# Announcing carry copies by the Exp that follows them, in a running log-sum-exp kernel

**Chip, cores, metric.** One core of a Trainium2 chip. The metric is the device time of one execution in microseconds; medians of several runs are quoted, and the profile is of one execution, whose span is some 1.7 us shorter than the device time. A run counts as slow when it is over 1.5% above the fastest run of the same kernel.

## The reference

A running log-sum-exp along the sequence, for 8 x 4096 x 2048 float32:

```python
out[:, 0, :] = x[:, 0, :]
for t in range(1, S):
    mx = np.maximum(out[:, t - 1, :], x[:, t, :])
    out[:, t, :] = mx + np.log(np.exp(out[:, t - 1, :] - mx) + np.exp(x[:, t, :] - mx))
```

It is the logarithm of a prefix sum of exp(x), and the kernel computes it so.

## The kernel before

The work is 64 tiles of 512 sequence rows (128 partitions, 4 rows each, 2048 columns, 4.19 MB). Six buffers `ti` hold tiles, each worked on in place: load, Exp, prefix sum, Ln, store. Everything is done in two column halves, h = 0 and 1. The last row of a tile is carried into the next through the tile `rs`: ACT copies partitions 96 to 127 into `rs`, then VectorE overwrites all but partition 127 with the new tile's sums of rows, and a matmul with a triangle turns `rs` into the offsets that VectorE adds ("join"). So VectorE's write of `rs` must come after ACT's copy; this order is what the change re-announces.

```python
# SyncE: loads
take(sp, stored[n], 16)                 # wait for the buffer's store, subtract
load(x_v[...], n)                       # ... loaded[n] += 16

# ACT
def exp(n, h, rows=slice(0, R)):
    t = ti[n % NI]
    if h == 0:
        take(act, loaded[n % NI], 16)   # an event instruction: wait and subtract
    act.activation(t[:, rows, half(h)], t[:, rows, half(h)], ACT.Exp).then_inc(exps[h], 1)

def copy(n, h, turn):
    act.activation(
        rs[P - 32:, half(h)], ti[n % NI][P - 32:, R - 1, half(h)], ACT.Copy
    )._wait_ge(joined[h], turn + 1).then_inc(moved, 1)
    event(act, [(moved, 2 * turn + h + 1)], [(copied[h], "sem-add-imm", 1)])

def step(n, turn, early=False):
    copy(n - 1, 0, turn)
    if early:                           # only for the last tile
        ln(n - 1, 0)
    exp(n, 0)
    exp(n, 1)
    copy(n - 1, 1, turn)
    if not early:
        ln(n - 1, 0)
    ln(n - 1, 1)                        # then the store of tile n - 1

# VectorE
def local(n, h):                        # sums of rows, three adds
    dve.tensor_add(...)._wait_ge(exps[h], n + 1).then_inc(chain[h], 1)
    dve.tensor_add(...)._wait_ge(chain[h], 3 * n + 1).then_inc(chain[h], 1)
    dve.wait_ge(copied[h], n + 1)
    dve.tensor_add(rs[:P - 1, cols], ...)._wait_ge(chain[h], 3 * n + 2).then_inc(sums[h], 1)

def join(n, h):                         # add the offsets from PSUM, two adds
    dve.tensor_add(...)._wait_ge(ahead[h], n + 1).then_inc(chain[h], 1)
    dve.tensor_add(...)._wait_ge(chain[h], 3 * n + 3).then_inc(joined[h], 1)
# per tile: local(n, 0), local(n, 1), join(n, 0), join(n, 1)
# ... (matmuls, loops over tiles, semaphore clean-up, launch)
```

The softmax here doesn't subtract the row's maximum and nothing guards it: scores larger than these inputs give would overflow.

## Time and profile before

| | before |
|---|---|
| median of the first three runs | 1250.54 us (1250.41 to 1250.74) |
| VectorE, ACT busy | 84%, 84% |
| two DMA queues, share of 16 engines | 49.9% + 49.8% |
| bytes moved, mean rate | 536.96 MB, 430 GB/s |
| store to store on ACT, first 290 us / later | 17.26 us / 19.4 us |

A line of a timeline is: start in us, duration, engine, source line, operation, output<-input, count (neighbours are merged, so "x2" with 7.12 us are two Exp halves of 3.6 us), and in brackets the idle time before it with its releaser. "ACTq" is ACT's sequencer, here issuing a store or taking a semaphore. The prediction below shows the lines.

### The profile page before, as it was taken

How to read it: one execution, taken by the hardware profiler on the slowest of the kernel's cores; microseconds unless marked ns; L12 is line 12 of the kernel's file. 1: busy time of each engine (PE TensorE's matmuls, PEld its weight loads, DVE VectorE, ACT ScalarE, POOL GpSimd, SP SyncE). 2: the span in 40 equal slices, each digit the busy share in tenths (PEclk: the TensorE clock that was granted, in tenths of full speed). 3: DMA queues.
4: the chain of work that ended last, by engine and by line, in shares of the span. 5: the costliest groups of instructions: out<-in, count | busy, mean ns of one | idle time of the engine just before them, and what ended most of it. 6: DMA issues, size and time to landing. Idle time of an engine off the chain costs nothing. (4 is left out here: it accounts for less than half of the span.)

```text
span 1249.0 us, 3085 instructions
## 1 busy us (share of the span) xinstructions
PE 385.3 (31%) x512; PEld 131.3 (11%) x512; DVE 1044.3 (84%) x640; ACT 1046.2 (84%) x385; POOL 1.0 (0%) x7
## 2 busy tenths in 40 slices
PE   1332333323323323233232331423323234142230
PEld 0110111101101101011010010101101101010010
DVE  4999999998888888888888888888888888888881
ACT  3999999998888888888888888888888888888892
POOL 0000000000000000000000000000000000000000
PEclk9666666666667576666665756666667565666665
DMA  9999999999999999999999999999999999999998
GB/s 403 420 437 434 425 434 435 434 434 428 432 436 437 433 428 432 435 436 433 429 432 434 437 433 428 432 436 436 433 430 431 436 436 433 430 430 437 436 432 348
DMA packets 18726, 536.96 MB, mean 430 GB/s; under 512 B 2080, under 2 KB 2080, under 8 KB 2080
## 3 DMA queue, kind: packets, MB, share of 16 engines
q1 hardware_dynamic: 9360, 268.44, 49.9%
q10 hardware_dynamic: 9360, 268.44, 49.8%
q8 instruction: 4, 0.07, 0.0%
q14 instruction: 2, 0.02, 0.0%
HBM read 268.44 MB, written 268.44 MB: 430 GB/s over the span
## 5 line engine op out<-in xcount | busy, mean ns | idle before, releaser
L215 PE MATMUL ps<-rs,before 128*128 128x512 f32 (+1 forms) x512 | 385.3, 905 | 831.7 <-DVE rs L240 831.0
L142 ACT ACTIVATE ti<-ti 128x4096 f32<-128x4096 f32 (+1 forms) x128 | 452.5, 3582 | 109.2 <-ACTq L63 109.2
L155 ACT ACTIVATE ti<-ti 128x4096 f32<-128x4096 f32 x129 | 456.3, 3583 | 12.9 <-DVE ti L250 4.6
L246 DVE TENSOR_TENSOR ti<-ti,ps 128x3072 f32<-128x3072 f32 x128 | 428.8, 3350 | 10.6 <-PE ps L215 10.3
L233 DVE TENSOR_TENSOR ti<-ti 128x1024 f32<-128x1024 f32 x128 | 156.4, 1222 | 155.9 <-ACT ti L142 155.9
L215 PEld LDWEIGHTS ps<-rs,before 128*128 128x128 f32 (+1 forms) x512 | 131.3, 285 | 1084.8 <-DVE rs L240 975.1
L148 ACT ACTIVATE rs<-ti 32x1024 f32<-32x1024 f32 x126 | 132.6, 1052 | 52.9 <-DVE ti L250 39.1
L240 DVE TENSOR_TENSOR rs<-ti 127x1024 f32<-127x1024 f32 x128 | 156.8, 1225 | 4.4
L250 DVE TENSOR_TENSOR ti<-ti 128x1024 f32<-128x1024 f32 x128 | 156.8, 1225 | 4.4
L236 DVE TENSOR_TENSOR ti<-ti 128x1024 f32<-128x1024 f32 x128 | 156.8, 1225 | 4.4
L184 ACT ACTIVATE ti<-ti 128x4096 f32<-128x4096 f32 x1 | 3.6, 3616 | 6.3 <-ACTq L63 6.3
L35 ACT ACT_TABLE_LOAD x1 | 1.3, 1283 | 0.8 <-PEq L283 0.8
L107 POOL TENSOR_SCALAR_AFFINE_SELECT before<-before 128x128 f32<-128x128 f32 x1 | 0.3, 294 | 0.1
L101 POOL TENSOR_SCALAR_AFFINE_SELECT before<-before 128x128 f32<-128x128 f32 x1 | 0.3, 294 | 0.1
L98 POOL MEMSET before<- 128x128 f32 x1 | 0.2, 205 | 0.5 <-SPq L81 0.5
L283 POOL MEMSET const-bfloat16-1.0<- 128x1 bf16 x1 | 0.1, 102 | 0.0
L283 POOL MEMSET const-uint8-127<- 128x1 uint8 x1 | 0.1, 102 | 0.0
L283 POOL MEMSET const-float32-0.0<- 128x1 f32 x1 | 0.1, 99 | 0.3 <-issue 0.3
L283 POOL MEMSET const-float32-1.0<- 128x1 f32 x1 | 0.1, 99 | 0.0
## 6 DMA issues: line engine op xcount, KB each, us to landing
ti<-in_x_dram SPq DMA_DIRECT2D x63, 4096.0 KB, 26.5
out_dram<-ti ACTq DMA_DIRECT2D x63, 4096.0 KB, 54.6
ti<-in_x_dram SPq DMA_DIRECT2D x2, 2048.0 KB, 9.5
out_dram<-ti ACTq DMA_DIRECT2D x2, 2048.0 KB, 18.1
```

Of the source, the lines that this page charges most:

```text
L35: nc.scalar.preload_act_table_set("natural_log_exp_and_others")
L142: act.activation(t[:, rows, half(h)], t[:, rows, half(h)], ACT.Exp).then_inc(exps[h], 1)
L148: act.activation(rs[P - 32:, half(h)], ti[n % NI][P - 32:, R - 1, half(h)], ACT.Copy)._wait_ge(joined[h], turn + 1).then_inc(moved, 1)
L155: act.activation(t[:, rows, half(h)], t[:, rows, half(h)], ACT.Ln).then_inc(logs, 1)
L184: act.activation(ti[0][:, 0:2, :], ti[0][:, 0:2, :], ACT.Exp)
L215: m = pe.matmul(ps[n % 2][:, sl], before[:k, :], rs[:k, sl], start=True, stop=True,)
L233: dve.tensor_add(t[:, 1, cols], t[:, 0, cols], t[:, 1, cols])._wait_ge(exps[h], n + 1).then_inc(chain[h], 1)
L236: dve.tensor_add(t[:, 2, cols], t[:, 1, cols], t[:, 2, cols])._wait_ge(chain[h], 3 * n + 1).then_inc(chain[h], 1)
L240: dve.tensor_add(rs[:P - 1, cols], t[:P - 1, 2, cols], t[:P - 1, 3, cols])._wait_ge(chain[h], 3 * n + 2).then_inc(sums[h], 1)
L246: dve.tensor_add(t[:, 0:3, cols], t[:, 0:3, cols], ps[n % 2][:, cols].unsqueeze(1).to_broadcast([P, 3, HALF]),)._wait_ge(ahead[h], n + 1). ...
L250: dve.tensor_add(t[:, 3, cols], t[:, 2, cols], t[:, 3, cols])._wait_ge(chain[h], 3 * n + 3).then_inc(joined[h], 1)
L283: nc = _bacc.Bacc("TRN2", target_bir_lowering=False, num_devices=1)
```

## The change

The intent is to have fewer instructions for synchronization. Where the Exp half comes behind the copy of the same half on ACT, the Exp's own semaphore already tells VectorE that the copy is done. So the second copy is moved in front of the second Exp, and the event instruction, the semaphore `copied` and VectorE's wait for it go. The Ln halves, which overwrite what the copies read, now wait for the copies' own semaphore `moved`.

```diff
-        exps, chain, sums, ahead, joined, copied = (
+        exps, chain, sums, ahead, joined = (
 ...
                     )._wait_ge(joined[h], turn + 1).then_inc(moved, 1)
-                    event(act, [(moved, 2 * turn + h + 1)], [(copied[h], "sem-add-imm", 1)])
 ...
-                def ln(n, h, rows=slice(0, R)):
+                def ln(n, h, ready, turn, rows=slice(0, R)):
                     ...
-                    ).then_inc(logs, 1)
+                    )._wait_ge(ready, turn).then_inc(logs, 1)
 ...
                     if early:
-                        ln(n - 1, 0)
+                        ln(n - 1, 0, moved, 2 * turn + 1)
                     exp(n, 0)
+                    copy(n - 1, 1, turn)
                     exp(n, 1)
-                    copy(n - 1, 1, turn)
                     if not early:
-                        ln(n - 1, 0)
-                    ln(n - 1, 1)
+                        ln(n - 1, 0, moved, 2 * turn + 1)
+                    ln(n - 1, 1, moved, 2 * turn + 2)
 ...
-                    dve.wait_ge(copied[h], n + 1)
 ...
-                        take(dve, copied[h], tiles)
```

(Cut: GpSimd's first increments of `copied`, and the two waits for `joined` at the end, which move into the Ln calls.)

More of the change, by code (lines that the diff above doesn't have):

```diff
@@ L89 @@
         loaded, stored = sems("loaded", NI), sems("stored", NI)
-        exps, chain, sums, ahead, joined, copied = (
-            sems(s, 2) for s in ("exps", "chain", "sums", "ahead", "joined", "copied")
+        exps, chain, sums, ahead, joined = (
+            sems(s, 2) for s in ("exps", "chain", "sums", "ahead", "joined")
         )
@@ L110, in _ @@
                 ).then_inc(shaped, 1)
-                for h in range(2):
-                    g.sem_inc(copied[h], 1)
             @block.sync
@@ L198, in _ @@
                 turn = NT - 1 - first
-                act.wait_ge(joined[0], turn + 1)
-                ln(NT - 1, 0)
-                act.wait_ge(joined[1], turn + 1)
+                ln(NT - 1, 0, joined[0], turn + 1)
                 done = 2 * turn + 1
                 for rows in LAST:
-                    ln(NT - 1, 1, rows)
+                    ln(NT - 1, 1, joined[1], turn + 1, rows)
                     done += 1
```

## The prediction

> **What bounds the kernel now.** I read the page first, then the list of waits, then the ACT timeline of one tile in the middle, then stretches of time at the end. The work is 64 tiles of 4.19 MB, each loaded, worked on in place in one of six buffers, and stored.
>
> ```profile
> span 1249.0 us, 3085 instructions
> ...
> PE 385.3 (31%) x512; PEld 131.3 (11%) x512; DVE 1044.3 (84%) x640; ACT 1046.2 (84%) x385; POOL 1.0 (0%) x7
> ...
> DMA  9999999999999999999999999999999999999998
> ...
> q1 hardware_dynamic: 9360, 268.44, 49.9%
> q10 hardware_dynamic: 9360, 268.44, 49.8%
> ```
>
> The reader is to see that no engine is above 84%, while the DMA row is full in 39 of 40 slices and the two queues (loads, stores) together took 49.9 + 49.8 = 99.7% of the time of the 16 DMA engines. 536.96 MB in 1249.0 us is 430 GB/s. The DMA is the bound.
>
> ```profile
> DVE ti L233 <- ACT ti L142: 155.9, 64, 15.2
> ...
> ACT ti L142 <- ACTq L63: 109.2, 63, 2.4
> ```
>
> The columns are us in total, times, longest. Line 63 is the helper that takes a semaphore; in front of an Exp that semaphore is the one of the load. So ACT waits 109 us for loads, and VectorE in turn 156 us for the Exp: slack of both engines.
>
> ```profile
> 305.76 0.34 ACTq L173 DMA_DIRECT2D out_dram<-ti  x1
> 306.15 1.05 ACT L148 ACTIVATE rs<-ti 32x1024 f32<-32x1024 f32 x1 [0.55 <-DVE ti L250]
> 309.51 7.12 ACT L142 ACTIVATE ti<-ti 128x4096 f32<-128x4096 f32 x2 [2.31 <-ACTq L63]
> 316.66 1.05 ACT L148 ACTIVATE rs<-ti 32x1024 f32<-32x1024 f32 x1
> 317.83 7.12 ACT L155 ACTIVATE ti<-ti 128x4096 f32<-128x4096 f32 x2
> 325.12 0.34 ACTq L173 DMA_DIRECT2D out_dram<-ti  x1
> ```
>
> One tile on ACT, mid-kernel: first carry copy, 2.31 us for the load, both Exp halves, second copy, both Ln halves, store. From store to store it is 325.12 - 305.76 = 19.36 us. The DMA needs 2 x 4.194 MB / 433 GB/s (the rate in the stretch from 290 to 1200 us) = 19.4 us for a tile. They agree: the transfers set the pace. Until about 290 us it is otherwise: the six loads given at the start are ahead, ACT runs from store to store in 17.26 us (61.70 to 78.96) with only 0.2 us of load wait, and the DMA share is 1.00 all the same (433 GB/s from 60 to 290 us), because stores pile up behind it.
>
> ```profile
> ti<-in_x_dram SPq DMA_DIRECT2D x63, 4096.0 KB, 26.5
> out_dram<-ti ACTq DMA_DIRECT2D x63, 4096.0 KB, 54.6
> ```
>
> The last column is the median from issue to landing: 26.5 + 54.6 = 81.1 us, or 81.1 / 19.4 = 4.2 tiles in transfer at any time. Six buffers make 116 us a round, so 35 us are left for the arithmetic of a tile. The store queue is some 2.8 tiles deep: a store given a microsecond later waits a microsecond less.
>
> **What the Trainium skill says.** "Perfetto Trace Analysis", section "Identifying the Most-Contended Engine": for DMA one should judge by the bandwidth used, as occupancy of 16 engines misleads. Here both say the same, 430 GB/s and 99.7%. "DMA: Bandwidth & Descriptors", section "Where 436 GB/s comes from", gives 435.2 GB/s as the ceiling of the ports, and says that between HBM and SBUF about 358 GB/s of HBM bind before it. The trace agrees with the first (430 mean, slices up to 437) and contradicts the second. The same page, section "Issuing engines are not separate DMA queues", says transfers issued by several engines share the 16 DMA engines; the shares of the two queues above, adding to 99.7%, agree. "VectorE: DVE Perf Modes", section "The DRAIN you can't avoid", measured that a semaphore after each operation costs nothing extra there. The trace agrees for VectorE: the adds of lines 233, 236 and 240 start at 313.16, 314.42 and 315.68, so the gap in front of line 240, where the wait to be removed stands, is the same 0.03 us as in front of line 236, where none stands.
>
> **The change part by part.**
> (a) VectorE loses 128 waits for the copies. By the row just read each costs 0.00 us. It also loses some subtractions at the end of each round of six tiles. Gain on VectorE: about nothing.
> (b) ACT loses 126 event instructions behind the copies. Copy to Ln: 316.66 + 1.05 = 317.71 to 317.83, a gap of 0.12 us where back-to-back ACT work has 0.02 to 0.03. So about 0.1 us each, two a tile, 63 tiles: 126 x 0.1 = 12.6 us of ACT idle. The one before the first Exp lies inside the load wait (or merges with it: 0.21 us where no load is awaited). None of it is on the path: ACT then waits longer for the load.
> (c) The second copy moves from behind the second Exp half to in front of it. Its total work on ACT is the same (1.05 us). The first Exp ends when it did, the second ends 1.05 + 0.03 = about 1.1 us later, the Ln halves start where they did, less the 0.1 of (b). So the stores of a tile in the steady part are issued at the same time or 0.1 us sooner.
> (d) VectorE feels the later second Exp. Its three adds of half 0 start when the first Exp ends and take about 3.7 us; the next half was ready at once (3.56 us after), and will be ready 1.08 us later, so VectorE idles about 0.9 to 1.0 us there. The joins move 1 us later. Is it paid for? In VectorE's timeline of the same tile the join of half 0 ends at 304.80 + 1.22 = 306.02 against a load at 309.4: 3.4 us, less the copy's 1.05, are room. And the join of half 1 ends at 309.33 + 1.23 = 310.56; with 1.0 us it is 311.6, before the first Exp's end at 313.1, where the moved copy needs it. So nothing slips further: VectorE waits 1.0 us less before half 0 and 1.0 us more before half 1.
> (e) In the first part, where the engines set their own pace, a new loop closes: second Exp, adds of half 1 (3.75), join of half 0 (4.6), copy (1.05 and 0.1 to 0.2 of hand-over), first Exp (3.6), copy (1.08), second Exp (3.6) = 17.8 to 17.9 us against 17.26 now. That is still below the DMA's 19.4. The read-ahead is used up more slowly: it was 230 us / 17.26 = 13 tiles at 2.1 us gained each; at 1.5 to 1.6 us gained, about 18 tiles, to some 380 us. The DMA stays full, so 0 us.
> (f) The end. The last tile's second Exp, the joins and the two last stores come about 1.0 us later.
>
> ```profile
> 1225.95 0.34 ACTq L173 DMA_DIRECT2D out_dram<-ti  x1
> ...
> 1228.27 0.34 ACTq L173 DMA_DIRECT2D out_dram<-ti  x1
> ```
> ```profile
> 1200.00:1228.00 28.00, 5.48 (x8) 1.85 (x8) 19.69 (x12) 22.72 (x9) 0.00 (x0) 0.63 1.00 432
> 1228.00:1249.00 21.00, 0.00 (x0) 0.00 (x0) 0.00 (x0) 0.24 (x1) 0.00 (x0) 0.50 0.72 311
> ```
>
> The last two numbers of a stretch are DMA share and GB/s. After 1228 us, 21 x 311 = 6.5 MB still move, and from 1225.95 to 1228 some 2 x 0.43 = 0.9 MB; the two last stores are 4.2 MB together. So when the first of them was issued, 6.5 + 0.9 - 4.2 = 3.2 MB stood before it, 7.5 us of transfer. A delay of 1.0 us uses part of this and leaves no hole.
> Sum: (a) 0, (b) 0, (c) 0, (d) 0, (e) 0, (f) 0. The time stays at 1250.5 us.
>
> **Rivals.**
> First, ACT as the bound, as its 84% and the short chain at the end (ACT and DVE work back to 1183 us) might suggest: then 12.6 us of removed gaps would show, 1250.5 - 12.6 = 1238 us, 1% less. Against it: the 109 us that ACT waits for loads, and the full DMA row.
> Second, the moved copy as a new serial wait: if joins of half 1 came after the first Exp, ACT would stand and both engines would fall into one chain. At my 17.9 us a tile there are 1.5 us of room; had I missed over 1.5 us a tile the kernel would be slower by 64 us for each further one: at 20.5 us a tile it would be about 1250 + 64 x 1.1 = 1320 us. For it speaks only that the new loop alternates between the engines; its terms are all measured, and an error of 1.5 us in six is unlikely.
> Third, the end: if the last stores were not backed by a queue, the 1.0 us of (f) would be added whole: 1251.5 us.
> Fourth, another mix of loads and stores changes the DMA rate. The slices vary from 425 to 437 GB/s; a shift of 0.2% of the mean would be 2.5 us either way. I can't derive a direction.
>
> **Range and chances.** I take 1250.5 us. The runs of before spread by 0.3 us; the third and fourth rival give 1 to 2.5 us. Range 1248.5 to 1253.0. Faster by over 2% would need under 1225.5, a mean of 438 GB/s even without any start and end, above every slice of the row: 0.005. Slower by over 2% means the second rival: 0.015. Within 2%: 0.98.
>
> **What would show it.** The DMA row stays full with 430 GB/s over the span. VectorE's waits for the Exp (line 233) rise from 64 to about 127 times with a sum still near 156 us, the new ones of about 1 us. The copy-to-Ln gap of 0.12 us is gone. ACT's wait for loads in mid-kernel stays at 2.3 us; the first part runs at 17.8 to 17.9 us a tile and lasts till about 380 us. The last store is issued about 1 us later with the span the same. Wrong would be: holes in the DMA row, a load wait near zero in mid-kernel, or waits of the second copy for the join of half 1.

## The result

The changed kernel is correct. It took 1250.34 us (median of four runs: 1250.27, 1250.32, 1250.35, and one slow, 1269.64); the kernel before, on the same chip, 1250.47 us. The ratio of the fast runs is 0.9999, with a 95% interval of 0.9979 to 1.0019. A ratio here is the mean time of one kernel's fast runs over that of the other's in the same rounds, so not quite the ratio of the medians.

The page of the changed kernel, its span, DMA row and DMA total:

```profile
span 1248.6 us, 2807 instructions
...
DMA  9999999999999999999999999999999999999998
...
DMA packets 18726, 536.96 MB, mean 430 GB/s; under 512 B 2080, under 2 KB 2080, under 8 KB 2080
```

There are 278 instructions less than the 3085 of before, and the DMA row is as full. Its waits (us in total, times, longest):

```profile
DVE ti L229 <- ACT ti L138: 168.3, 127, 15.4
...
ACT rs L147 <- DVE ti L245: 92.1, 63, 10.2
ACT ti L138 <- ACTq L63: 75.6, 45, 1.7
```

The kernel before had, for the wait of the first copy:

```profile
ACT rs L148 <- DVE ti L250: 39.1, 53, 10.5
```

VectorE waits for an Exp 127 times instead of 64. ACT's first copy waits for the join 92.1 us instead of 39.1, and its Exp for loads 75.6 instead of 109.2: part of the slack has moved from the load wait to the join wait. The ACT timeline of one tile in mid-kernel:

```profile
714.07 0.34 ACTq L171 DMA_DIRECT2D out_dram<-ti  x1
715.23 1.05 ACT L147 ACTIVATE rs<-ti 32x1024 f32<-32x1024 f32 x1 [1.32 <-DVE ti L245]
717.99 3.62 ACT L138 ACTIVATE ti<-ti 128x4096 f32<-128x4096 f32 x1 [1.71 <-ACTq L63]
721.63 1.05 ACT L147 ACTIVATE rs<-ti 32x1024 f32<-32x1024 f32 x1
722.71 3.62 ACT L138 ACTIVATE ti<-ti 128x4096 f32<-128x4096 f32 x1
726.23 7.11 ACT L153 ACTIVATE ti<-ti 128x4096 f32<-128x4096 f32 x2
733.50 0.34 ACTq L171 DMA_DIRECT2D out_dram<-ti  x1
```

Store to store is 733.50 - 714.07 = 19.43 us, the same as before within the scatter of single tiles. The load comes 717.99 - 714.07 = 3.92 us after the store's issue (in the kernel before, from the lines in the prediction: 309.51 - 305.76 = 3.75), and from there to the next store it takes 15.51 us (before: 15.61). Only what lies inside is arranged differently. In the first part the stores come at 61.73, 79.47, 97.22 and so on, 17.74 us apart, up to about 345 us.

The stretches at the end of the changed kernel (last two numbers: DMA share and GB/s), and its last two stores:

```profile
1200.00:1228.00 28.00, 5.83 (x9) 1.85 (x8) 21.62 (x13) 21.35 (x8) 0.00 (x0) 0.68 1.00 431
1228.00:1249.00 21.00, 0.00 (x0) 0.00 (x0) 0.00 (x0) 2.43 (x2) 0.00 (x0) 0.50 0.73 315
```
```profile
1228.55 0.34 ACTq L171 DMA_DIRECT2D out_dram<-ti  x1
...
1230.88 0.34 ACTq L171 DMA_DIRECT2D out_dram<-ti  x1
```

The last stores are issued 2.6 us later than before, and the span still ends 0.4 us earlier.

### The profile page after: what moved, and what is told of

It is laid out like the page before. It is cut to its first block, busy times and chain, and to the rows that moved or that the text cites. A ratio compares the mean times of both kernels' runs of the same rounds, so it can differ in the third digit from the quotient of the medians.

```text
span 1248.6 us, 2807 instructions
## 1 busy us (share of the span) xinstructions
PE 418.3 (33%) x512; PEld 133.3 (11%) x512; DVE 1045.1 (84%) x640; ACT 1046.2 (84%) x385; POOL 1.0 (0%) x7
## 5 line engine op out<-in xcount | busy, mean ns | idle before, releaser
L211 PE MATMUL ps<-rs,before 128*128 128x512 f32 (+1 forms) x512 | 418.3, 964 | 801.3 <-DVE rs L235 801.2
L138 ACT ACTIVATE ti<-ti 128x4096 f32<-128x4096 f32 (+1 forms) x128 | 459.4, 3590 | 77.6 <-ACTq L63 75.6
L147 ACT ACTIVATE rs<-ti 32x1024 f32<-32x1024 f32 x126 | 132.6, 1052 | 93.6 <-DVE ti L245 92.1
```

The costliest lines, as they stand in the source:

```text
L147: act.activation(rs[P - 32:, half(h)], ti[n % NI][P - 32:, R - 1, half(h)], ACT.Copy)._wait_ge(joined[h], turn + 1).then_inc(moved, 1)
L211: m = pe.matmul(ps[n % 2][:, sl], before[:k, :], rs[:k, sl], start=True, stop=True,)
```

## The experiments

The theory under test: the transfers pace the kernel, the change makes the loop of the engines longer (17.26 to 17.74 us a tile), and the transfers hide that. The main rivals: the two parts cancel (moving costs what dropping events gains); the engines' loop already paces, or never matters; the end is a chain of engines.

| run | us, median | runs | ratio to before (95%) |
|---|---|---|---|
| move alone | 1251.38 | 5 | 1.0006 (0.9993 to 1.0019) |
| events of half 0 alone | 1250.83 | 6 | 1.0010 (0.9998 to 1.0021) |
| changed, one extra copy a tile | 1250.69 | 4 | 1.0000 (0.9986 to 1.0015) |
| changed, two extra copies a tile | 1306.38 | 4 | 1.0445 (1.0430 to 1.0460) |
| stores cut: before | 1146.12 | 4 | 0.9163 |
| stores cut: changed | 1169.82 | 4 | 0.9353 |
| stores cut: move alone | 1187.86 | 4 | 0.9496 |
| stores cut: events of half 0 alone | 1135.01 | 4 | 0.9074 |
| changed, end later by 2 dummies | 1251.42 | 4 | 1.0015 (0.9998 to 1.0032) |
| changed, end later by 5 dummies | 1252.27 | 7 | 1.0011 (0.9997 to 1.0025) |
| changed, end later by 8 dummies | 1258.12 | 4 | 1.0059 (1.0042 to 1.0075) |
| transfers alone | 1247.71 | 4 | 0.9976 (0.9959 to 0.9992) |

### Each part alone

The move without dropping anything:

```diff
                     exp(n, 0)
-                    exp(n, 1)
                     copy(n - 1, 1, turn)
+                    exp(n, 1)
```

> The kernel before with the second carry copy moved in front of the second Exp half; the event instructions and VectorE waits stay. Theory (transfers bind, both parts of the change are off the path): 1250.4 us within 0.1%, the DMA row full, and up to some 350 us a pace of about 18.0 us a tile (the 17.74 us of the changed kernel plus some 0.2 to 0.3 us of event gaps that now lie in the loop). Rival (two parts that cancel: the move costs and the dropped events pay for it): slower than before by about 126 x 0.1 = 12 us, near 1262 us.

And the dropping where no move is needed, for half 0:

```diff
-                    event(act, [(moved, 2 * turn + h + 1)], [(copied[h], "sem-add-imm", 1)])
+                    if h == 1:
+                        event(act, [(moved, 2 * turn + 2)], [(copied[1], "sem-add-imm", 1)])
...
-                    dve.wait_ge(copied[h], n + 1)
+                    if h == 1:
+                        dve.wait_ge(copied[1], n + 1)
```

(Cut: the first increment and the subtractions of `copied` for half 0, and a wait for `moved` in front of the early Ln of the last step.)

> The kernel before with event and wait dropped for half 0 alone, where the Exp half already stands behind the copy; the order of instructions is untouched. Theory (transfers bind): 1250.4 us within 0.1%; in the first part about 17.1 us a tile instead of 17.26. Rival (cancelling parts): the dropped events gain 63 x 0.1 to 0.2 us, so 1238 to 1244 us.

Both take the time of the kernel before. The stores of the first part came 18.02 us apart with the move alone and 17.08 us with the events of half 0 gone, as expected, and neither shows in the end. So the two parts don't cancel; each is hidden by itself, as the runs with stores cut, below, show with the price of each. The second kernel had two longer runs, 1252.16 and 1255.5 us, beside four between 1250.38 and 1251.14 (see the end of the section on the end).

### How much room the loop has

One or two needless copies of the carry's size behind the moved copy, into a spare tile:

```diff
+                    for j in range(EXTRA if h == 1 else 0):
+                        act.activation(
+                            spare[P - 32:, :], ti[n % NI][P - 32:, R - 1, half(1)], ACT.Copy
+                        )._wait_ge(moved, PER * turn + 2 + j).then_inc(moved, 1)
```

(Cut: the spare tile, and `PER`, the number of copies a tile, in the other waits for `moved`.)

> The changed kernel with one needless carry-sized copy (1.05 us) a tile behind the moved copy, so the loop of the engines grows from 17.74 to about 18.9 us a tile, still under the 19.43 us of the transfers. Theory: 1250 to 1252 us. Rival (the loop ACT - VectorE - ACT is already what paces the steady part): slower by 63 x 1.1 = 69 us, near 1320 us.

> The same with two needless copies a tile: loop about 20.0 us, now over the 19.43 us of the transfers. Theory: the bound changes over, stores at 20.0 us a tile from the first at 44 us: 44 + 62 x 20.0 + some 25 for the end = about 1309 us (1300 to 1320), and the DMA row no longer full. Rival (engines never on the path, whatever they cost): 1250 us. Rival (loop paces already): 1250 + 63 x 2.2 = 1389 us.

The first run paid 1.09 us a tile (18.83 us from store to store for the first 53 steps, then 19.4 us for the eight that follow) and lost nothing. The second ran at 19.91 us a tile and lost 4.45%. The DMA totals of the page tell which side each is on, first one extra copy, then two:

```profile
DMA packets 18726, 536.96 MB, mean 430 GB/s; under 512 B 2080, under 2 KB 2080, under 8 KB 2080
...
ACT ti L141 <- ACTq L66: 6.1, 9, 1.3
```
```profile
DMA packets 18726, 536.96 MB, mean 412 GB/s; under 512 B 2080, under 2 KB 2080, under 8 KB 2080
...
ACT ti L141 <- ACTq L66: 1.2, 1, 1.2
```

With two copies a load is awaited once in the whole kernel, and the rate falls to 412 GB/s. That wait is at the start. With one copy, eight of the nine waits come after the 53 steps at 18.83 us: through these the engines spaced the stores, with no wait for a load, and the total still did not grow. So a load wait near zero is no sign of a loss by itself; the transfers that were queued ahead have to be used up first. The two runs bracket the turning point between 18.83 and 19.91 us. It is not the 19.43 us of the transfers: the second run lost 1306.38 - 1250.69 = 55.7 us over 62 steps, 0.90 us a step, so an estimate from it is 19.91 - 0.90 = 19.0 us. (The kernels without a loss take 18.9 us a step in the mean of these 62, as their first steps are quicker.) This refutes both rivals about the loop: that it paced already, and that it never matters.

### The change where the transfers don't pace

The stores of all but the last tile carry only half of the rows; the results are wrong (rows of the output stay unwritten). All else is as in the four kernels named.

```diff
-                def store(n, dst, done, rows=slice(0, R)):
+                def store(n, dst, done, rows=slice(0, 2)):
```

> The kernel before, storing only half of the rows of all tiles but the last (a wrong result on purpose), so that a tile needs about 14.6 us of transfers and the engines set the pace throughout. Theory: the pace of the first part of the trace, 17.26 us a tile plus 0.74 us every six tiles, holds to the end: 44.4 + 62 x 17.38 + 12.7 + 10 = about 1145 us (1138 to 1152).

> The changed kernel with the same cut of the stores. Theory (the change lengthens the loop of the engines and the transfers hid it): 17.74 us a tile: 44.4 + 62 x 17.74 + 13.9 + 10 = about 1168 us (1160 to 1176), 2% slower than the kernel before with the same cut. Rival (the change is neutral on the engines too): the same as the kernel before with the cut, 1145 us. Rival (it makes the engines faster, by the 12.6 us of dropped gaps): 1133 us.

> Only the moved copy, events and waits kept, stores cut. Theory: all of the loss is from the move, and the dropped events win a part back: loop about 18.0 us a tile, about 1185 us (1178 to 1192), slower than the changed kernel with the cut. Rival (the loss in the first part comes from dropping the events): about 1145 us.

> Only the half-0 events and waits dropped, no move, stores cut. Theory: the gap between first copy and first Exp falls from 0.21 to about 0.03 us, ACT paces at 17.08 us a tile plus 0.74 every six: about 1134 us (1128 to 1142), the fastest of the four. Rival (an event costs nothing, as waits on VectorE do): 1145 us.

All four hit their ranges. Without the cover of the transfers the change costs 1169.82 - 1146.12 = 23.7 us (2.1%). Most of it is 0.36 us a step and not 17.74 - 17.26 = 0.48: in the kernel before every sixth step takes some 17.95 us, so its mean over 62 steps is 17.38 us, while in the changed kernel nearly all take 17.74 us. The move alone costs 41.7 us; dropping the events in the moved order wins 18.0 us of that back. Dropping the half-0 events without the move wins 11.1 us and is the fastest of the four. The gap on ACT between the first copy and the Exp shows where it is won; first the kernel before, then the half-0 one, both with stores cut:

```profile
705.98 1.05 ACT L148 ACTIVATE rs<-ti 32x1024 f32<-32x1024 f32 x1 [0.55 <-DVE ti L250]
707.24 7.12 ACT L142 ACTIVATE ti<-ti 128x4096 f32<-128x4096 f32 x2 [0.21 <-ACTq L63]
```
```profile
715.87 1.05 ACT L147 ACTIVATE rs<-ti 32x1024 f32<-32x1024 f32 x1 [0.55 <-DVE ti L251]
716.95 3.62 ACT L141 ACTIVATE ti<-ti 128x4096 f32<-128x4096 f32 x1
```

705.98 + 1.05 = 707.03, so the Exp stood 0.21 us behind the copy; without the event it is 0.03 us. 62 tiles x 0.18 us = 11.2 us, the whole gain. The taking of the load semaphore, which stands in both, then shows no cost beyond this 0.03 us.

### The end

Needless copies of 2048 elements into a free PSUM tile in front of the last Ln pieces of the changed kernel delay its last two stores. The edit, for two, five or eight of them (k):

```diff
+                for j in range(k):
+                    act.activation(
+                        ps[0][:].rearrange("p (a b) -> p a b", a=2),
+                        ti[(NT - 1) % NI][:, 0:2, half(1)], ACT.Copy
+                    )._wait_ge(*((joined[1], turn + 1) if j == 0 else (pad, j))).then_inc(pad, 1)
                 for rows in LAST:
```

> The changed kernel with two needless copies of 2048 elements into PSUM on ACT in front of the last Ln quarter tiles, some 4 us, so that the two last stores are issued some 4 us later. Theory (transfers queued at the end cover a delay of about 4.9 us, worked out for the changed kernel as 6.3 MB still to move at 1228.55 us less the 4.2 MB of the two last stores): 1250 to 1251 us. Rival (the end is a chain of engines and the last stores count at once): 1254.4 us.

> The same with eight needless copies, some 15.5 us. Theory: 4.9 us of it are covered, the rest counts: about 1261 us (1258 to 1264). Rival (end chain counts at once): 1266 us. Rival (the end is covered far more): 1250 us.

With two, the first of the last stores was issued 3.7 us later (1232.24), and the profiled run took 1250.34 us with the span of the changed kernel, 1248.6 us. The other three runs took 1251.19, 1251.65 and 1255.16 us, so the median of 1251.42 us is 0.4 above the range foretold; the scatter leaves a loss of up to a microsecond open, but not the 4 us of the rival. With eight, the store was issued 15.6 us later (1244.15) and the span grew by 8.1 us. So 7.5 us were covered: more than the 4.9 us that I had worked out. The stretches of that run show why:

```profile
1232.00:1234.00 2.00, 0.00 (x0) 0.00 (x0) 0.00 (x0) 1.97 (x2) 0.00 (x0) 0.50 0.65 279
1234.00:1236.00 2.00, 0.00 (x0) 0.00 (x0) 0.00 (x0) 1.97 (x2) 0.00 (x0) 0.50 0.08 33
1236.00:1240.00 4.00, 0.00 (x0) 0.00 (x0) 0.00 (x0) 3.94 (x3) 0.00 (x0) 0.50 0.04 16
```

The mean queue does run dry at about 1233.4 us, which is 4.9 us after 1228.55, as worked out. But a share of 0.08, little more than one engine in sixteen, works on until 1238. That it is one engine, the trace shows in two ways. From 1235.0 us on the packets come one after another, 32 KB in 1.21 us each, to 1238.7 us. And each transfer raises its semaphore 16 times, as often as there are engines: of the 16 increments of the last whole store, fifteen come within 2.1 us and the sixteenth 3.6 us later. After the gap, the 16 of each of the two last stores come within 0.16 us. In the undelayed changed kernel, where there is no gap, fifteen come within 1.6 us and the last 2.4 us later, up to the end, and the end waits for it (25 GB/s from 1244 to 1246 us). A gap in front of the last stores lets the laggard catch up. A last run put a number on it:

> As the two runs with a late end, with five needless copies, so that the last stores are issued some 9.8 us later than in the changed kernel. The run with eight showed 15.6 us of delay for 8.1 us of span, so 7.5 us were covered, more than the 4.9 us worked out from the mean of the queues. New theory (the end is that of the one DMA engine that lags: there the queue is longer than the mean): 9.8 - 7.5 = 2.3 us of loss, about 1252.6 us, span 1250.9. Old figure (4.9 us covered): 4.9 us of loss, about 1255.2 us. Rival (end chain counts at once): 1260 us.

Its median was 1252.27 us, with the new theory's 1252.6 and not the 1255.2 of the old figure. Its profiled run was one of the longer ones (1262.22 us; another took 1257.65), so its profile says nothing about the cover.

That profile does say something about the longer runs. From 800 to 1200 us its DMA share is 1.00 as in the changed kernel, but the rate is 429 GB/s instead of 433, and the 16 increments of one transfer spread over up to 13 us instead of 4: more single packets took over 1.3 times their usual time (357 against 54 in the changed kernel), and the stores came up to 20.5 us apart. So in that run the transfers themselves were slower; why stays open. The slow run of the result (1269.64 us) may be of the same kind: its granted clock, 0.624, is no lower than that of fast runs (0.622 with eight dummies). All 38 runs of the kernel before lie between 1250.01 and 1251.51 us, while of the 34 runs of the changed kernel and of its variants that the transfers bound, five lie over 3.5 us above the median of their own kernel. Whether the change makes such runs likelier was not tested; one of the five kept the order of before.

### The transfers by themselves

The kernel with loads and stores alone, stores issued as soon as a load lands:

```diff
-            (Exp, copies, Ln, VectorE, TensorE, GpSimd)
+                def store(n, dst):
+                    take(act, loaded[n % NI], 16)
+                    act.dma_start(out=dst, in_=ti[n % NI][:]).then_inc(stored[n % NI], 16)
```

> Loads and stores alone, the same sizes, queues and six buffers, no arithmetic (a wrong result on purpose: the input is stored). Theory (transfers bind): 537 MB at 433 GB/s = 1239 us plus start and end: 1243 to 1248 us, within 0.6% of both kernels. Rival (the engines hold the transfers back): clearly lower, under 1230 us.

It took 1247.71 us. All of the arithmetic, with its order and its waits, thus adds 3 us (0.24%) to what these transfers need without it (here the last tile goes out in one store instead of two). An arrangement of the engines that keeps the sizes, queues and buffers has hardly more than this to win, so no version was built to beat both kernels. Another order or size of the transfers was not tried.

## Why the prediction was right, and where it was off

The time (1250.5 foretold, 1250.34 measured) and the reason hold: the transfers pace, shown by the two runs around the threshold and by the transfers alone. By its steps:

- (a) VectorE's waits cost nothing: held. After the change, with no wait in front of the third, the adds of lines 229, 232 and 235 still start 1.26 us apart.
- (b) ACT's events: the size was half right. I gave 0.1 us for each; the one behind the second copy (0.12 us to the next instruction, 0.03 left without it) costs that, the one in front of the first Exp 0.18 us. Being off the path, it made no difference in the end.
- (c) From the first Exp to the store 0.1 us less: held (15.61 to 15.51 us).
- (d) VectorE idles 0.97 us before half 1, as foretold. But I wrote that ACT's load wait stays at 2.3 us and VectorE's waits sum to 156 us. I had the joins one microsecond later in the same paragraph and didn't carry it on to the first copy, which waits for a join: it came 0.8 us later after the store, and the load wait behind it shrank to 1.7 us. VectorE's waits summed to 168 us.
- (e) 17.8 to 17.9 us a tile foretold, 17.74 measured; end of the first part near 345 us instead of 380. The count of some 18 tiles was right (17 steps), but I counted them from 60 us and not from the first store at 44 us. The mechanism held, and the stores-cut pair shows its full price, 23.7 us.
- (f) The last stores came 2.6 us later, not 1.0. The term that was too small: the step before the last has an Ln in front of the Exp instead of a load wait, so the later join of that tile isn't absorbed (0.9 us), the transfers stood 0.8 us later already, and the later second Exp adds 1.0 us. That it is covered held, but with less to spare than I had thought: the 7.5 us of the prediction are for a store issued at 1225.95 us, and by the same sum 4.9 us are left at 1228.55. That 7.5 us were measured there is a coincidence; the rest comes from the lagging engine, which the prediction did not have.

The number, 0.2 us off, is no measure of these steps: the cover hid the errors of (b), (d) and (f), and right and wrong sizes alike led to the same time. Their worth was shown only by the runs that took the cover away.

Of the rivals, ACT as the bound and the moved copy as the pacing wait are refuted, and so is an uncovered end. The second rival was given too much room: the 1.5 us at 17.9 us a tile were reckoned to the 19.4 us of the transfers, where the turning point is near 19.0. At 19.91 us its formula gives 1250 + 64 x 0.5 = 1282 us, and the run with two copies took 1306.38. A shift of the DMA rate by another mix didn't appear: 433 GB/s in the stretch from 290 to 1200 us in both kernels.

## What to carry to other kernels

Where the DMA row is full and the engines wait for loads, as here, a change to the synchronization has to be judged twice: by the time, which may not move, and by the pace of a stretch in which the engines set it (here the first 300 us), because that pace tells the room left for the next change. The change dropped 278 instructions and yet used up 0.36 of some 1.6 us of room a tile (mean steps of 17.38 and 17.74 us against a turning point estimated at 19.0), since it moved a copy into a loop between two engines. Once that loop sets the pace, each further copy in it costs its whole length (1.09 us measured). The cheap test of such a claim is a dose: add the disputed cost once and twice, and see where the time turns; it can turn earlier than the transfers' own pace says.

## What the Trainium skill lacked or had wrong

- "DMA: Bandwidth & Descriptors", section "Where 436 GB/s comes from", says that about 358 GB/s of HBM bind between HBM and SBUF. With this core's program alone, loads and stores together ran at 433 GB/s for 900 us, and 431 GB/s over the whole span without arithmetic. The 435.2 GB/s of the ports in the same section is the figure that fits (single slices of the profile read up to 437). The page itself puts it right a few lines earlier, in the note under its measured table, where the 358 GB/s are the share when both cores of a pair stream; the sentence lacks that condition.
- None of the pages read gives the cost of an event instruction (wait for one semaphore, raise another) between two activations. Behind a copy that it must wait out, it cost 0.18 us in front of an Exp (gap 0.21 to 0.03 us) and 0.09 us in front of an Ln (0.12 to 0.03 us). A taken semaphore that was already there cost nothing visible.
- "DMA: Bandwidth & Descriptors" has it that two of the 16 DMA engines are usually slower, but not how far one falls behind in a long stream of loads and stores. Here the mean queue was dry at 1233.4 us while one engine worked on to 1238.7 us, so 7.5 us of delay were covered at the end where the mean queue promised 4.9.
- Not explained by any page read: some runs of kernels bound by transfers are longer with no lower granted clock (1255.16, 1255.5, 1257.65, 1262.22 and perhaps 1269.64 us among runs near 1250 to 1252). The one that was profiled moved 429 GB/s at a full DMA share. None of the 16 runs with stores cut strayed by more than 1.1 us from its median.
